# Operands of later pairs kept unsplit in DRAM, split when they are loaded at the border, and prepared at every second tick

## The chip, the cores and the metric

One core of one Trainium2 chip. The time is device microseconds of one execution of the program; the lower the better. TensorE (PE in the profile) multiplies, VectorE (DVE), ScalarE (ACT) and GpSimd (POOL) work element by element, and SyncE (SP) issues all DMAs here.

## The reference, cut to what matters

One layer of a streaming encoder on 2048 prompt tokens, 16 meta tokens and 8 x 16 sample tokens, all in float32. A mixer (retention heads and a convolution module) comes first; what the change touches is the MLP behind it.

```python
x = x + rms_norm(mix, g_post_mix)
h = rms_norm(x, g_pre_mlp)
f = jnp.square(jax.nn.relu(h @ w_mlp_in)) @ w_mlp_out      # 1024 -> 4096 -> 1024
x = x + rms_norm(f, g_post_mlp)
```

## The kernel before, in words

**Splits.** Every float32 operand of a matmul is split into a rounded part (fp32r, made by an ACT copy) and the rest (made by a subtraction on POOL or DVE); `split` (L325) does both. A product is then three matmuls: high by high, high by low, low by high (`mm3`, L451; `product`, L1125).

**Groups, pairs, blocks.** The tokens lie in six groups; the mixer works group by group. The MLP works on three pairs of groups, `FG = [(1, 2), (3, 4), (5, 0)]`, numbered G = 0, 1, 2, with 2 x 384, 2 x 384 and 2 x 320 columns (`NH2`). For each pair it goes through 16 blocks `b` of the hidden layer (`plan`, L88; the loop at L1257). A block computes layer 1 as a 2 x 2 block product in seven products P1 to P7 instead of eight (Winograd's form): seven left operands made of sums of weight blocks (`wp`, `fetch_product`, L268), and seven right operands made of sums of activation blocks (`hops`, called `op` in the profile). Each product is 12 matmuls (4 k, three each) and accumulates in three PSUM tiles `mm`. Between the products stand the 16 tiles of layer 2 of the block before (`l2_tile`, L1189, six matmuls each). In the last block of pairs 0 and 1 layer 2 of that block follows at once (`end_layer2`, L1204, 16 more tiles), and block 0 of the next pair has products alone. This change of pairs is called the border here.

**Weights.** For pair 0 the seven `wp` of a block are summed on POOL, split on ACT (L298) and POOL (L299) and stored to DRAM (L319, `wprod`); for pairs 1 and 2 they are loaded from there (L273). Layer 2's weights are loaded and split anew for each pair (`split_unit`, L254: L258 to L261). Both share nine buffers, and `next_unit` (L305) fetches ahead as far as they go.

**Right operands.** Seven tiles, each of eight column blocks: four k high, four k low. Their places (`home`, L541) are tiles that the mixer used before. The operands of pair 0 are made in place by `make_h2` with `put_home` (L547, L576). Those of pairs 1 and 2 are prepared during the pair before by the generator `prologue` (L1065): first `mlp_in` for each of the two groups (L476: residual add, two RMS norms, each in a pass of eight steps that loads one block of 128 channels, with a norm between; results `x1d` and `hd` in DRAM), then `make_h2` with `put_dram` (L585): per k it loads `hd` into two `st` tiles (L555), forms four differences on POOL (L561), splits all seven parts into `so` tiles (L327, L328) and stores them to `opd` (L592). In the last block of the pair, right behind product x, the finished operand x of the next pair is loaded into its place by one DMA (L1142).

**What sets the order.** The program is written by generators in queues; `tick` (L367) is called after each product and after each layer 2 tile (23 times in a block with 16 tiles) and takes one step from the queue `mlp`, where `prologue` is put after block 1, and in this stage two from `norm`, which holds the epilogues. A yield of `WAIT` ends the tick for its queue. Before the last block `mlp` is drained. A planner in the framework then places the instructions in the engines' queues by a simulated timeline, in which steps of `mlp` are set back by 100 places (`later`, L337) and those of `norm` by none; each engine's queue runs in its order. `st` tiles come from a pool of three (L1056), `s` tiles from a pool of five (L473), the PSUM tiles of `mlp_in`'s norms from the pool `aux` that layer 2 uses as well.

Of the kernel before, what the change touches and what calls it, by code (L numbers as in the profile page):

```python
# [12 lines left out]
F32 = mybir.dt.float32  # L13
F32R = mybir.dt.float32r
I32 = mybir.dt.int32
AF = mybir.ActivationFunctionType
ALU = mybir.AluOpType
# [3 lines left out]
P = 128  # L21
# [60 lines left out]
P1, P2, P3, P4, P5, P6, P7 = range(7)  # L82
ORDER = (P1, P2, P6, P5, P7, P3, P4)
NG = 3
NH2 = [384, 384, 320]
# [66 lines left out]
def build(nc, T):  # L152
    lg = _log_gamma()
    with tile.TileContext(nc, schedule_with_timeline_sim=True) as tc, ExitStack() as top:
# [12 lines left out]
        dram = ep(tc.tile_pool(name="dram", bufs=1, space=DRAM))  # L167
# [157 lines left out]
        def split(src, hi, lo, eng=None):  # L325

            nc.scalar.activation(out=hi, in_=src, func=AF.Copy)  # L327
            (eng or nc.gpsimd).tensor_tensor(out=lo, in0=src, in1=hi.bitcast(F32), op=ALU.subtract)  # L328
# [4 lines left out]
        queues = {"head": deque(), "norm": deque(), "conv": deque(), "mlp": deque()}  # L333

        rate = {"norm": 1, "conv": 5, "mlp": 1}
# [3 lines left out]
        def advance(gen, off):  # L339

            tc.cur_priority += off
            try:
                return next(gen)
            finally:
                tc.cur_priority -= off

        def step(name, n):
            q = queues[name]
            while n > 0 and q:
                try:  # L350
                    if advance(q[0], later["ln" if q[0].__name__ == "conv_norm" else name]) == WAIT:
                        return
                    n -= 1
                except StopIteration:
                    q.popleft()

        heads_done = {}

        def tick_heads():
            hq = queues["head"]  # L360
            for gen in list(hq):
                try:
                    advance(gen, later["head"])
                except StopIteration:
                    hq.remove(gen)

        def tick():  # L367
            tick_heads()
            step("norm", rate["norm"])
            step("conv", rate["conv"])  # L370
            step("mlp", rate["mlp"])

        def drain(*names):
            while any(queues[n] for n in names):
# [85 lines left out]
        NM = max(g["N"] for g in LAY)  # L460
# [6 lines left out]
        hd = [dram.tile([KT, P, 2 * n], F32, name=f"hd{G}") for G, n in enumerate(NH2)]  # L467
        stqs = []

        def st_tile():  # L470
            return stqs[0].tile([P, 2 * NM], F32, tag="st", name="st")

        def s_tile(N):  # L473
            return np_.tile([P, WM], F32, tag="s", name="s", bufs=SB)[:, :N]
# [61 lines left out]
        OPS = (P1, P2, P6, P5, P7, P3, P4)  # L536
        HOME = {P1: "hhi", P2: "hlo", P6: "chi", P5: "clo", P7: "x", P3: "hhi", P4: "hlo"}
        hops, h2_made = {}, set()
        opd = [None] + [dram.tile([7, P, 8 * n], F32, name=f"opd{n}") for n in NH2[1:]]

        def home(G, x):  # L541
            pool = {"h": hp, "c": catp, "x": xp}[HOME[x][0]]
            t = pool.tile([P, 8, NM if pool is catp else WM], F32R, tag=HOME[x], name=f"op{x}")
            hops[G, x] = t[:, :, :NH2[G]]
            return hops[G, x]
# [36 lines left out]
                yield  # L582
            return put

        def put_dram(G, eng):  # L585
            n = NH2[G]

            def put(x, k, part):
                t = stqs[0].tile([P, 2, NM], F32R, tag="so", name="so", bufs=2)[:, :, :n]
                split(part, t[:, 0], t[:, 1], eng)  # L590
                yield
                nc.sync.dma_start(opd[G][x].rearrange("p (h k n) -> p h k n", h=2, k=4)[:, :, k], t.bitcast(F32))  # L592
            return put


        mstack = ExitStack()
# [199 lines left out]
        part = {}  # L796
# [268 lines left out]
        def prologue(G):  # L1065
            for gi in FG[G]:
                yield from mlp_in(gi)
            yield from make_h2(G, OPS, nc.gpsimd, put_dram(G, nc.gpsimd))

        def segments(G, c):  # L1070

# [46 lines left out]
        def layer1(G, b):  # L1118

            n = NH2[G]  # L1120
            fh = [fp.tile([P, FB, NM], F32R, tag=f"fh{c}", name=f"fh{c}") for c in range(2)]
            fl = [fp.tile([P, FB, NM], F32R, tag=f"fl{c}", name=f"fl{c}") for c in range(2)]
            banks = {}

            def product(x, key, first, last=True):  # L1125
                while (G, x) not in h2_made:
                    step("norm", 1)
                w = next_unit("p", G, (b, x))
                ops = hops[G, x]
                if first:  # L1130
                    banks[key] = mmp.tile([P, 512], F32, tag="mm", name="mm")[:, :n]
                ps = banks[key]
                for k in range(4):
                    hi, lo = w[:, k * P:(k + 1) * P], w[:, 512 + k * P:512 + (k + 1) * P]
                    start = first and k == 0
                    nc.tensor.matmul(ps, hi, ops[:, k, :n], start=start, stop=False, skip_group_check=not first)  # L1136
                    nc.tensor.matmul(ps, hi, ops[:, 4 + k, :n], start=False, stop=False, skip_group_check=not first)  # L1137
                    nc.tensor.matmul(ps, lo, ops[:, k, :n], start=False, stop=(k == 3), skip_group_check=not first)  # L1138
                if b == NFB - 1 and G < NG - 1:

                    t = home(G + 1, x)
                    nc.sync.dma_start(t.bitcast(F32), opd[G + 1][x].rearrange("p (k n) -> p k n", k=8))  # L1142
                    h2_made.add((G + 1, x))
                return ps

            def copy(ps):
                t = x1p.tile([P, NM], F32, tag="sn", name="sn", bufs=2)[:, :n]
                nc.scalar.activation(out=t, in_=ps, func=AF.Copy)
                return t

            def added(ps, t):
                r = yop.tile([P, NM], F32, tag="yo", name="c", bufs=3)[:, :n]
                nc.vector.tensor_tensor(out=r, in0=ps, in1=t, op=ALU.add)
                return r

            def out(i, c, src, r=None):

                if r is None:
                    r = yop.tile([P, NM], F32, tag="yo", name="r", bufs=3)[:, :n]
                    nc.scalar.activation(out=r, in_=src, func=AF.Relu)  # L1160
                    nc.vector.scalar_tensor_tensor(out=r, in0=src, scalar=0.0, in1=r, op0=ALU.max, op1=ALU.mult)
                else:
                    nc.scalar.activation(out=r, in_=r, func=AF.Relu)
                    nc.scalar.activation(out=r, in_=r, func=AF.Square)
                split(r, fh[c][:, i, :n], fl[c][:, i, :n])

            def run():
                s1 = copy(product(P1, "y", True))
                yield
                r = added(product(P2, "z", True), s1)  # L1170
                out(0, 0, None, r)
                yield
                u2 = copy(product(P6, "y", False))
                yield
                product(P5, "w", True)
                yield
                u3 = copy(product(P7, "y", False))
                r = added(banks["w"], u3)
                out(1, 1, None, r)
                yield  # L1180
                r = added(product(P3, "w", False), u2)
                out(0, 1, None, r)
                yield
                out(1, 0, product(P4, "y", False))
                yield

            return (fh, fl), run()
# [69 lines left out]
        for G, b, steps in plan():  # L1257
            if b == 0:
                drain("norm")
                ya = {(c, r): x1p.tile([P, 4, NM], F32, tag=f"ya{c}{r}", name=f"ya{c}{r}")  # L1260
                      for c in range(2) for r in range(2)}
            rate["norm"] = 2
            if b == NFB - 1:
                drain("mlp")
            cur, run = layer1(G, b)
            w = {}
            for what, x in steps:
                if what == "p":
                    next(run)
                    tick()  # L1270
                elif what == "w":
                    w[x] = next_unit("l2", G, x)
                else:
                    q, o, c = x
                    l2_tile(G, b - 1, c, q, o, w[b - 1, q], prev, ya)
                    tick()
            if b == 1 and G + 1 < NG:
                queues["mlp"].append(prologue(G + 1))
            if b == NFB - 1:
                if G + 1 < NG:  # L1280
                    end_layer2(G, b, [w[b, q] for q in range(FB)], cur, ya)
                else:
                    last_layer2(G, [w[e, q] for e in (b - 1, b) for q in range(FB)], (prev, cur), ya)
            prev = cur
# [59 lines left out]
```

## Time and profile before

| what | us |
|---|---|
| median of 3 runs | 2510.81 |
| lowest and highest of them | 2507.74, 2510.89 |
| the profiled execution, its own time | 2508.38 |
| its span, first to last instruction | 2506.6 |

The MLP of pair 0 begins at about 975 us of the span, the border to pair 1 lies at about 1485 to 1535 us, that to pair 2 at about 2010 to 2060 us. The page gives for every engine its busy time, and a chain of what released what, followed back from the last instruction. A window row gives, for one stretch, the busy time of each engine and in brackets how many instructions ran in it, then TensorE's granted clock as a share of 2.4 GHz, the busy share of the 16 DMA engines and what they moved. A matmul's shown time overlaps with its neighbours', so the count of matmuls in a stretch tells more than their busy time. A group row gives the busy time, the mean of one in ns, and behind the second bar the idle time just before, with what ended it.

### The profile page before, as it was taken

Reading aid. Unit: us, or ns where it says so; the run is one execution under the profiler, and the core shown is the slowest. Engines: PE = TensorE matmul, PEld = TensorE weight load, DVE = VectorE, ACT = ScalarE, POOL = GpSimd, SP = SyncE. Lnnn points to the kernel's source line nnn. Section 1 sums busy time; section 2 is a strip of 40 time slices with the busy share of each in tenths; the row PEclk is TensorE's granted clock in tenths of the full one; section 3 lists DMA queues with packets and bytes.
Section 4 is the critical chain, followed back from the end, with each engine's and each line's share of the span. In section 5 each row is a group of like instructions: output and inputs, shape, how many; then the busy total and the mean of one; then the engine's idle time right before and its main releaser. Section 6 shows DMA issues by size and latency. Waiting matters only on the chain. (4 is left out here: it accounts for less than half of the span.)

```text
span 2506.6 us, 40862 instructions
## 1 busy us (share of the span) xinstructions
PE 2383.7 (95%) x14538; PEld 2340.0 (93%) x14538; DVE 1473.2 (59%) x3292; ACT 894.8 (36%) x1896; POOL 1111.9 (44%) x1024
## 2 busy tenths in 40 slices
PE   7889999998999998998999999989999999999997
PEld 6789999998999997987999999989999999999996
DVE  8879797896987955555433337554333355333335
ACT  5424424123233234444444444333422233333232
POOL 6625212131232115775999764435622226233324
PEclk8999999998999999998999999999999999999999
DMA  9888778898597778676877569778744487555552
GB/s 335 319 284 318 254 271 268 247 326 273 196 306 261 245 255 336 230 258 229 285 265 273 187 231 358 256 231 270 262 152 151 152 298 270 184 177 187 175 189 90
DMA packets 257628, 617.43 MB, mean 246 GB/s; under 512 B 32144, under 2 KB 116880, under 8 KB 256528
## 3 DMA queue, kind: packets, MB, share of 16 engines
q1 hardware_dynamic: 257424, 614.82, 71.9%
q8 instruction: 115, 1.88, 0.3%
q14 instruction: 89, 0.73, 0.1%
HBM read 463.69 MB, written 151.02 MB: 245 GB/s over the span
## 5 line engine op out<-in xcount | busy, mean ns | idle before, releaser
L1136 PE MATMUL mm<-op,wp 128*128 128x384 f32 (+1 forms) x1344 | 444.6, 333 | 22.6 <-ACT wp L298 10.1
L1138 PE MATMUL mm<-op,wp 128*128 128x384 f32 (+1 forms) x1344 | 443.6, 331 | 6.2 <-POOL wp L299 6.2
L1137 PE MATMUL mm<-op,wp 128*128 128x384 f32 (+1 forms) x1344 | 443.9, 330 | 1.4 <-DVE op L328 1.4
L260 POOL TENSOR_TENSOR wlo<-raw,whi 128x512 fp32r<-128x512 f32 x244 | 320.7, 1334 | 270.2 <-PE mma L456 117.5
L745 DVE SCALAR_TENSOR_TENSOR cv<-ext,par,cv 128x384 f32<-128x384 f32 (+1 forms) x720 | 379.2, 568 | 1.7
L454 PE MATMUL mm<-hhi,whi 128*128 128x384 f32 (+2 forms) x992 | 336.2, 339 | 18.7 <-ACT whi L259 9.7
L456 PE MATMUL mm<-hhi,wlo 128*128 128x384 f32 (+2 forms) x992 | 333.9, 338 | 10.7 <-POOL wlo L260 5.8
L455 PE MATMUL mm<-hlo,whi 128*128 128x384 f32 (+2 forms) x992 | 332.4, 335 | 0.3
L1201 DVE TENSOR_TENSOR ya<-mmc,ya 128x384 f32<-128x384 f32 (+1 forms) x344 | 181.8, 535 | 241.5 <-PE mmc L456 240.5
L1201 DVE TENSOR_TENSOR ya<-mma,ya 128x384 f32<-128x384 f32 (+1 forms) x344 | 183.5, 534 | 231.6 <-PE mma L456 231.1
L328 POOL TENSOR_TENSOR fl<-c,fh 128x384 fp32r<-128x384 f32 (+1 forms) x144 | 144.5, 1005 | 324.4 <-ACT fh L327 303.7
L1136 PEld LDWEIGHTS mm<-op,wp 128*128 128x128 f32 x1344 | 255.8, 191 | 30.4 <-ACT wp L298 13.5
L1138 PEld LDWEIGHTS mm<-op,wp 128*128 128x128 f32 x1344 | 256.0, 191 | 8.6 <-POOL wp L299 8.5
L1137 PEld LDWEIGHTS mm<-op,wp 128*128 128x128 f32 x1344 | 256.5, 191 | 2.5 <-DVE op L328 2.2
L456 PE MATMUL mmc<-fh,wlo 128*128 128x384 f32 (+1 forms) x768 | 252.2, 330 | 6.0 <-POOL wlo L260 6.0
L454 PE MATMUL mma<-fh,whi 128*128 128x384 f32 (+1 forms) x768 | 252.4, 331 | 4.7 <-DVE ya L1201 2.4
L454 PE MATMUL mmc<-fh,whi 128*128 128x384 f32 (+1 forms) x768 | 251.4, 330 | 4.0 <-DVE ya L1201 3.2
L455 PE MATMUL mmc<-fl,whi 128*128 128x384 f32 (+1 forms) x768 | 251.9, 328 | 0.9 <-POOL fl L328 0.8
L455 PE MATMUL mma<-fl,whi 128*128 128x384 f32 (+1 forms) x768 | 251.6, 328 | 0.3 <-POOL fl L328 0.3
L456 PE MATMUL mma<-fh,wlo 128*128 128x384 f32 (+1 forms) x768 | 251.3, 327 | 0.4 <-POOL wlo L260 0.4
L454 PEld LDWEIGHTS mm<-hhi,whi 128*128 128x128 f32 x992 | 194.1, 196 | 21.2 <-ACT whi L259 11.1
L456 PEld LDWEIGHTS mm<-hhi,wlo 128*128 128x128 f32 x992 | 192.8, 195 | 15.0 <-POOL wlo L260 8.7
(237 smaller groups left out, 4810.4 us busy)
## 6 DMA issues: line engine op xcount, KB each, us to landing
wp<-wprod SPq DMA_DIRECT2D x224, 512.0 KB, 4.2
raw<-w SPq DMA_DIRECT2D x256, 256.0 KB, 4.1
whi<-wkeep_in SPq DMA_DIRECT2D x120, 512.0 KB, 5.9
wlo<-wkeep_in SPq DMA_DIRECT2D x120, 512.0 KB, 4.9
wprod<-wp SPq DMA_DIRECT2D x112, 512.0 KB, 4.4
whi<-wkeep_out SPq DMA_DIRECT2D x40, 512.0 KB, 6.3
wlo<-wkeep_out SPq DMA_DIRECT2D x40, 512.0 KB, 5.6
s<-yscr SPq DMA_DIRECT2D x80, 192.0 KB, 4.4
```

The source lines that it names most:

```text
L260: (nc.vector if i < 24 and i % 4 == 0 else nc.gpsimd).tensor_tensor(out=lo[:, c], in0=raw, in1=hi[:, c].bitcast(F32), op=ALU.subtract)
L328: (eng or nc.gpsimd).tensor_tensor(out=lo, in0=src, in1=hi.bitcast(F32), op=ALU.subtract)
L454: nc.tensor.matmul(ps, whi(k), ahi(k), start=(k == 0), stop=False)
L455: nc.tensor.matmul(ps, whi(k), alo(k), start=False, stop=False)
L456: nc.tensor.matmul(ps, wlo(k), ahi(k), start=False, stop=(k == nk - 1))
L745: nc.vector.scalar_tensor_tensor(out=o, in0=src(t), scalar=wt, in1=o, op0=ALU.mult, op1=ALU.add)
L1136: nc.tensor.matmul(ps, hi, ops[:, k, :n], start=start, stop=False, skip_group_check=not first)
L1137: nc.tensor.matmul(ps, hi, ops[:, 4 + k, :n], start=False, stop=False, skip_group_check=not first)
L1138: nc.tensor.matmul(ps, lo, ops[:, k, :n], start=False, stop=(k == 3), skip_group_check=not first)
L1201: last_y[0] = nc.vector.tensor_tensor(out=y, in0=ps, in1=y, op=ALU.add)
```

## The change

The seven operands of a later pair are no longer split and stored while the pair before runs. Four of them are differences, which `differences` forms on POOL and stores unsplit to `td`; the other three are blocks of `hd` as they are. In the last block, behind product x, a generator `reload` for operand x is put into the queue `norm`: it loads the four unsplit k blocks by two DMAs into two `st` tiles, then splits them into the operand's place, the copy on ACT, the subtraction in turn on POOL and DVE. The prologue is put into its queue after block 2 instead of block 1, and from then on `mlp` gets a step at every second tick.

```diff
+        ticks, slow = [0], [1]
...
-            step("mlp", rate["mlp"])
+            ticks[0] += 1
+            if ticks[0] % slow[0] == 0:
+                step("mlp", rate["mlp"])
...
-        opd = [None] + [dram.tile([7, P, 8 * n], F32, name=f"opd{n}") for n in NH2[1:]]
+
+        td = [None] + [dram.tile([4, 4, P, n], F32, name=f"td{n}") for n in NH2[1:]]
...
-        def put_dram(G, eng):
+        def differences(G):
+
             n = NH2[G]
-
-            def put(x, k, part):
-                t = stqs[0].tile([P, 2, NM], F32R, tag="so", name="so", bufs=2)[:, :, :n]
-                split(part, t[:, 0], t[:, 1], eng)
-                yield
-                nc.sync.dma_start(opd[G][x].rearrange("p (h k n) -> p h k n", h=2, k=4)[:, :, k], t.bitcast(F32))
-            return put
+            for k in range(4):
+                bs = {}
+                for r in range(2):
+                    t = st_tile()[:, :2 * n]
+                    nc.sync.dma_start(t, hd[G][k + 4 * r])
+                    bs[r, 0], bs[r, 1] = t[:, :n], t[:, n:]
+                yield
+                ts = []
+                for i in range(4):
+                    x, y = ((bs[0, 1], bs[0, 0]), (bs[1, 1], ts[0] if i == 1 else None), (bs[1, 1], bs[0, 1]),
+                            (bs[1, 0], ts[1] if i == 3 else None))[i]
+                    t = s_tile(n)
+                    nc.gpsimd.tensor_tensor(out=t, in0=x, in1=y, op=ALU.subtract)
+                    nc.sync.dma_start(td[G][i, k], t)
+                    ts.append(t)
+                    yield
+
+        def reload(G, x):
+
+            n = NH2[G]
+            t = home(G, x)
+            ld = []
+            for k in (0, 2):
+                src = {P1: lambda: hd[G][k:k + 2, :, :n], P2: lambda: hd[G][4 + k:6 + k, :, :n],
+                       P3: lambda: hd[G][4 + k:6 + k, :, n:], P5: lambda: td[G][0, k:k + 2],
+                       P6: lambda: td[G][1, k:k + 2], P7: lambda: td[G][2, k:k + 2],
+                       P4: lambda: td[G][3, k:k + 2]}[x]()
+                ld.append(st_tile()[:, :2 * n].rearrange("p (k n) -> p k n", k=2))
+                nc.sync.dma_start(ld[-1], src.rearrange("k p n -> p k n"))
+            yield
+            for k in range(4):
+                split(ld[k // 2][:, k % 2], t[:, k], t[:, 4 + k], nc.vector if k % 2 else nc.gpsimd)
+                if k == 3:
+                    h2_made.add((G, x))
+                yield
...
-            yield from make_h2(G, OPS, nc.gpsimd, put_dram(G, nc.gpsimd))
+            yield from differences(G)
...
-
-                    t = home(G + 1, x)
-                    nc.sync.dma_start(t.bitcast(F32), opd[G + 1][x].rearrange("p (k n) -> p k n", k=8))
-                    h2_made.add((G + 1, x))
+                    queues["norm"].append(reload(G + 1, x))
...
-            if b == 1 and G + 1 < NG:
+            if b == 2 and G + 1 < NG:
+                slow[0] = 2
                 queues["mlp"].append(prologue(G + 1))
```

## Rows read from the trace of the kernel before

**Rows 1.** The page: span, TensorE's busy time, chain that ended last by engine.

```profile
span 2506.6 us, 40862 instructions
...
PE 2383.7 (95%) x14538; PEld 2340.0 (93%) x14538; DVE 1473.2 (59%) x3292; ACT 894.8 (36%) x1896; POOL 1111.9 (44%) x1024
...
PE 27%; DMA 3%; POOL 1%; DVE 1%; issue 0%; ACT 0%; SPq 0%; DVEq 0%; ACTq 0%; POOLq 0%
```

**Rows 2.** Windows: 100 us in pair 0 and 100 us in pair 1, undisturbed.

```profile
core 0: us, PE busy (x) PEld busy (x) DVE busy (x) ACT busy (x) POOL busy (x), PEclk, DMA share, GB/s
...
1260.00:1360.00 100.00, 100.00 (x579) 100.00 (x578) 34.29 (x65) 48.10 (x98) 98.00 (x87) 1.00 0.74 264
...
1835.00:1935.00 100.00, 100.00 (x579) 100.00 (x578) 35.00 (x64) 28.40 (x56) 28.39 (x25) 1.00 0.46 148
```

**Rows 3.** Windows: stretches of the prologues of pair 1 and pair 2.

```profile
1035.00:1110.00 75.00, 73.40 (x414) 71.32 (x413) 42.76 (x82) 35.37 (x73) 55.84 (x49) 1.00 0.72 243
1110.00:1210.00 100.00, 82.62 (x389) 74.71 (x388) 53.42 (x98) 36.40 (x74) 61.68 (x54) 0.88 0.77 255
...
1560.00:1660.00 100.00, 97.08 (x547) 94.14 (x545) 61.56 (x118) 36.41 (x75) 44.00 (x40) 1.00 0.80 263
1660.00:1735.00 75.00, 64.30 (x335) 60.75 (x336) 37.14 (x82) 24.56 (x54) 32.07 (x34) 0.95 0.71 229
1785.00:1810.00 25.00, 22.88 (x132) 22.42 (x131) 7.33 (x14) 10.66 (x23) 15.26 (x17) 1.00 0.81 268
```

**Rows 4.** Groups of TensorE's matmuls, 1110 to 1210 us, with their waits.

```profile
L1136 PE MATMUL mm<-op,wp 128*128 128x384 f32 x60 | 23.7, 394 | 7.7 <-ACT wp L298 7.7
L1138 PE MATMUL mm<-op,wp 128*128 128x384 f32 x60 | 22.8, 386 | 3.0 <-POOL wp L299 3.0
...
L456 PE MATMUL mmc<-fh,wlo 128*128 128x384 f32 x30 | 11.2, 392 | 3.7 <-POOL wlo L260 3.7
```

**Rows 5.** The same groups, 1660 to 1735 us, then 1785 to 1812 us.

```profile
L1136 PE MATMUL mm<-op,wp 128*128 128x384 f32 x51 | 18.7, 366 | 8.3 <-DMA wp<-wprod 6.7 <-DVE st L397 1.6
...
L454 PE MATMUL mma<-fh,whi 128*128 128x384 f32 x12 | 4.1, 345 | 2.1 <-ACT fh L327 2.1
```

**Rows 6.** Groups of POOL and of ACT, 1200 to 1360 us: the splits into `so`.

```profile
L328 POOL TENSOR_TENSOR so<-s,so 128x384 fp32r<-128x384 f32 x16 | 17.4, 1094 | 0.0
L328 POOL TENSOR_TENSOR so<-st,so 128x384 fp32r<-128x384 f32 x12 | 13.0, 1082 | 0.0
...
L327 ACT ACTIVATE so<-s 128x384 fp32r<-128x384 f32 x16 | 8.3, 521 | 17.5 <-DMA opd<-so 15.9 <-POOL so L328 1.6
...
L327 ACT ACTIVATE so<-st 128x384 fp32r<-128x384 f32 x12 | 6.2, 519 | 4.6 <-DMA opd<-so 3.4 <-DMA st<-hd 1.3
```

**Rows 7.** DMA issues of the whole kernel: KB each, median us from issue to landing.

```profile
st<-hd SPq DMA_DIRECT2D x32, 384.0 KB, 5.6
opd<-so SPq DMA_DIRECT2D x28, 384.0 KB, 4.0
op<-opd SPq DMA_DIRECT2D x7, 1536.0 KB, 13.6
```

**Rows 8.** Tile `s` and line 561: ns of one (min/median/max), DVE and POOL.

```profile
L524 POOL TENSOR_TENSOR s<-s x48: 725/1013/1330, 504.5 to 1699.0; 128x384 f32<-128x384 f32 x40, 128x256 f32<-128x256 f32 x8
...
L522 DVE SCALAR_TENSOR_TENSOR s<-s,par,sw x32: 471/606/617, 1067.3 to 1696.7; 128x384 f32<-128x384 f32 x24, 128x256 f32<-128x256 f32 x8
...
L561 POOL TENSOR_TENSOR s<-st x16: 869/955/1136, 1201.6 to 1784.0; 128x384 f32<-128x384 f32 x8, 128x320 f32<-128x320 f32 x8
```

**Rows 9.** Pair 0's operands: their splits, then DVE's group and the window 985 to 1010.

```profile
L327 ACT ACTIVATE op<-s x16: 508/524/527, 930.4 to 1011.9; 128x384 fp32r<-128x384 f32 x16
L328 DVE TENSOR_TENSOR op<-s,op x16: 546/559/1357, 930.9 to 1012.5; 128x384 fp32r<-128x384 f32 x16
...
L327 ACT ACTIVATE op<-st x12: 507/517/528, 928.3 to 1006.3; 128x384 fp32r<-128x384 f32 x12
...
L328 DVE TENSOR_TENSOR op<-s,op 128x384 fp32r<-128x384 f32 x3 | 3.2, 1083 | 1.2 <-ACT op L327 1.2
...
985.00:1010.00 25.00, 17.53 (x73) 14.47 (x71) 18.90 (x16) 11.48 (x23) 25.00 (x18) 0.80 0.92 334
```

**Rows 10.** Window in pair 0 without a prologue.

```profile
1410.00:1435.00 25.00, 25.00 (x146) 25.00 (x145) 9.26 (x17) 11.39 (x22) 19.32 (x17) 1.00 0.63 209
```

**Rows 11.** Windows of 5 us around single waits of TensorE.

```profile
1115.00:1120.00 5.00, 2.15 (x9) 1.83 (x10) 0.26 (x1) 0.63 (x1) 2.65 (x3) 0.87 0.79 251
1120.00:1125.00 5.00, 4.67 (x15) 4.16 (x14) 2.55 (x5) 0.00 (x0) 3.02 (x3) 0.50 0.91 273
...
1640.00:1645.00 5.00, 3.47 (x20) 3.15 (x19) 4.87 (x11) 0.36 (x1) 2.68 (x2) 1.00 0.96 370
```

**Rows 12.** Windows of the two borders.

```profile
1485.00:1535.00 50.00, 50.00 (x288) 49.73 (x287) 25.70 (x50) 17.14 (x34) 15.81 (x14) 1.00 0.96 380
...
2010.00:2060.00 50.00, 50.00 (x293) 49.73 (x292) 23.61 (x46) 16.87 (x35) 14.16 (x13) 1.00 0.91 322
```

## The prediction

> **What bounds the kernel.** The page comes first: TensorE is busy 95% of the span, and the chain that ended last is mostly matmuls [rows 1]. So only time in which TensorE stands still, or runs slowly, can be won. Where that is, the windows of the MLP stage show. In an undisturbed stretch 100 us hold 579 matmuls of 384 columns, 0.1727 us each, beside no idle time at clock 1.00, in the first pair as in the second [rows 2]. A block `b` is 180 of them (84 in the products, 96 in layer 2), 31.1 us. Stretches in which the next pair's operands are prepared hold fewer [rows 3]. What is missing, against 5.79 per us, by 0.1727 us:
> - first prologue, group 3: 434 - 414 = 20, 3.5 us; group 4: 579 - 389 = 190, 32.8 us
> - second prologue, group 5: 579 - 547 = 32, 5.5 us; group 0: 434 - 335 = 99, 17.1 us; the end of its operands: 145 - 132 = 13, 2.2 us
>
> That is 61.1 us in all. TensorE's idle time in these five rows is 1.60 + 17.38 + 2.92 + 10.70 + 2.12 = 34.7 us; the other 26.4 us are matmuls at the lower clock (rows 3: granted 0.88 and 0.95 in the two worst). What it waits for is weights: in the first pair operands that ACT and POOL still have to split, in the second a `wp` load that SP issued late [rows 4, 5]. These engines' queues run in order, and the steps of `mlp_in` stand between: a load, then DVE, POOL, ACT and a store, each waiting for the one before. In group 4's stretch neither DVE, ACT nor POOL is busy two thirds of the time [rows 3]: it is blocked order, not a full engine.
>
> **What is removed.** For each later pair 28 ACT copies, 28 POOL subtractions and 28 stores of 384 KB and 7 loads of 1536 KB (a sixth less for the last pair) [rows 6, 7]. In the first prologue that is 14.5 us of ACT and 30.4 us of POOL, but it lies between 1200 and 1360 us, and from 1260 on TensorE loses nothing there though POOL is busy 98 of 100 us [rows 2, 6]: weights fetched ahead cover a full POOL. So the removal itself is worth the 2.2 us at 1785 to 1810, where TensorE waited for an `fh` split on ACT [rows 5]. If the cover goes, it is worth more; nothing here says so.
>
> **What is moved and thinned.** `mlp_in` is 28 steps a group (8, 2, 8, 2, 8), two groups; `make_h2` 4 x 8 = 32; `differences` 4 x 5 = 20. So 88 steps become 76, and at every second tick they take 152 ticks for 88. A block has 23 ticks: 6.6 blocks (206 us) for 3.8 (119 us). It begins one block later and ends around block 10, well ahead of the drain at block 15. The later start leaves the first blocks alone, where 73 of 145 matmuls were done in 25 us, 12.4 us missing [rows 9]; those wait for the first pair's own splits, so I count nothing, and up to a quarter, 3 us, for the range. In the middle pass of `mlp_in` one step costs DVE 0.61 and 0.56 us, POOL 1.01 us [rows 8, 9] (the second DVE operation is an add of the same width as the DVE splits, whose duration I take). At a step per tick (31.1 / 23 = 1.35 us) DVE gets 0.87 of its time on top of the 0.35 that the blocks need [rows 2], more than it has; POOL in the first pair gets 0.75 on top of 0.77 [rows 10]. At half the rate this is 0.43 + 0.35 on DVE and 0.37 + 0.77 on POOL, in a pass of eight steps a backlog of 3 us. A load is also issued one step ahead of its use, and a step becomes 2.7 us long.
>
> How much of the 61.1 us returns no row shows. Below: nothing (the waits keep their size; a loss I exclude, since each queue gets less in any stretch). Above: all of it. The nearest rows are the prologues' own first groups, same operations at the same rate, which lose 3.5 and 5.5 us before queues are behind. I take that each second group falls to its first group's loss: 2 x (3.5 + 5.5) = 18.0 us stay, **43.1 us return**. The clock's part goes with it: at 1640 to 1645 us a lone 1.53 us of idle time left the clock at 1.00, while at 1115 to 1125 idle time in close order brought it down to 0.50, which is 1.2 GHz [rows 11].
>
> The Trainium skill, "TensorE: Matmul & The Clock Gate", section "A second HAM failure mode: psum-queue depth-cycling", says that frequent short idles between groups of matmuls are enough to bring the lower clock, paid for again each time; the second of these rows agrees, the first does not. By it the same number of waits over twice the stretch would win nothing, and the sum would be 2512: rival 2.
>
> **What is added.** At each of two borders 14 loads, 28 ACT copies, 14 POOL and 14 DVE splits. ACT: 28 x 0.52 = 14.6 us; POOL 14 x 1.09 = 15.3 us; DVE 14 x 0.56 = 7.8 us, or 14 x 1.08 = 15.1 us as in the stretch where POOL was busy throughout [rows 6, 9]. The borders' 50 us leave ACT 33, POOL 34 and DVE 24 us free while TensorE has no idle time [rows 12]. So the price is not room but order. An operand's place is free once its product in the last block is done; a reload then stands on ACT and POOL in front of the `fh` and `fl` splits that layer 2 of the last block waits for, and its loads stand on SP in front of `wp` and `raw`. I take one reload in front of that split: 4 x 0.52 + 1.09 = 3.2 us a border, **6.3 us** for both; it could be nothing (the planner can put a product of the next pair there), or, if reloads come too slowly, 26 us a border (below). DMA gets lighter: 14 loads of 384 KB, 5.4 MB, in place of 7 of 1536 KB, 10.8 MB, at a border that had a DMA share of 0.96 [rows 12]; priced at nothing. `differences` keeps the 16 POOL differences of a pair [rows 8] and adds 16 stores of 192 KB; each waits on SP for its difference, with `wp` loads behind it, as the 28 stores waited for their splits.
>
> **Sum.** 61.1 - 18.0 - 6.3 = 36.8 us from the profiled execution's own 2508.4 us (span 2506.6 and 1.8 around it): 2471.6, said as **2472**. The median of the three runs, 2510.81, lies 2.4 us higher, inside what the sum can tell.
>
> **Rivals.**
> 1. *The waits keep their idle time, the clock alone comes back.* Every step blocks for its DMA's time however far apart steps are; 34.7 us of idle time stay but scattered, 26.4 return: 2508.4 - 26.4 + 6.3 = **2488**. For: every wait is a latency. Against: group 3 had the same steps and lost a tenth of group 4.
> 2. *Nothing returns.* The waits keep size and number, and the clock falls as often: 2508.4 - 2.2 + 6.3 = **2512**. It also comes out so if the planner, which places instructions by its own estimate of when they are ready, draws the thinned steps together again. For: the row with 0.50. Against: the lone gap there.
> 3. *The border is laid open: slower.* The only rows with 28 splits into these places, those of the first pair, took from 928 to 1012 us, 12 us an operand, and TensorE was busy 17.53 of the last 25 [rows 9]. At a border the reload of the first operand can begin 2 us into the last block, and the seventh is wanted at 31.1 + 16.6 (the last layer 2) + 12.4 = 60 us; that allows 8.3 us an operand. At 12 us the seventh is ready at 86: 26 us late, 52 for both, 2508.4 - 43.1 + 52 = **2517**, and up to 2535 with the lower clock and late first operands. Against: at the borders no block's `wp` are still to be split as at the start, the weights of the next pair being loaded, and the ticks issue an operand every 4.4 us. For: only three `st` buffers serve the loads, two an operand, so loads (5.6 us [rows 7]) and splits (2.1 us of ACT) may follow one another: 7.7 us, close under 8.3.
>
> **How the numbers follow.** Forecast 0.50, rival 1 0.20, rival 2 0.10, rival 3 0.20. The forecast's own range goes from 2444 (all 61.1 us back, no price, and 3 us of the start) to 2491 (two borders at 13 us, half the worst); with rival 1 and rival 2 the range is **2444 to 2513**, which leaves out about rival 3. About 0.2% (5 us) is what a measurement can tell from no change. Forecast and rival 1 are faster by more: 0.70; rival 2 is the same: 0.10; slower 0.20.
>
> **What would show it.** Right: no window of the prologues below 130 matmuls in 25 us, clock 1.00 from 1060 to 1480 us and in the second pair; `mlp_in` steps over some 200 us; TensorE's waits for `wp` in rows 4 and 5 under a third; the border windows at 140 or more in 25 us. Wrong: windows with 75 to 110 matmuls still there, only further apart (rivals 1, 2); TensorE waiting for ACT or DVE writing `op`, or for `st` loads, at the first block of a pair (rival 3).

## The result, and the profile after

| kernel | median us | lowest to highest | ratio to before (95% interval) |
|---|---|---|---|
| before | 2509.27 | 2507.70 to 2510.89 | |
| changed | 2470.64 | 2467.02 to 2475.32 | 0.9847 (0.9825 to 0.9868) |

2472 was forecast. The profiled execution of the changed kernel took 2468.89 us (span 2467.0), 39.5 us less than that of before (2508.38); 36.8 us were forecast.

The page of the changed kernel, next to [rows 1]: TensorE has the same 14538 matmuls, is busy 20.6 us less with them, and the span is 39.6 us shorter; so about half of the gain is idle time, and the rest a shorter busy time for the same matmuls.

```profile
span 2467.0 us, 40738 instructions
...
PE 2363.1 (96%) x14538; PEld 2327.8 (94%) x14538; DVE 1506.2 (61%) x3320; ACT 894.5 (36%) x1896; POOL 1092.7 (44%) x996
```

Where the 39.5 us went is a matter of counting matmuls, as with [rows 2, 3]. Two stretches that hold both prologues in either kernel, but for their first loads, 325 and 250 us, would hold 1882 and 1448 matmuls at 5.79 per us. First the kernel before:

```profile
1035.00:1360.00 325.00, 306.02 (x1667) 296.04 (x1666) 149.35 (x279) 142.52 (x287) 265.52 (x232) 0.96 0.75 260
1560.00:1810.00 250.00, 234.26 (x1301) 227.31 (x1300) 123.65 (x247) 90.68 (x192) 123.87 (x125) 0.99 0.78 256
```

The same windows of the changed kernel, then the worst stretch of before [rows 3] in it, and the two parts of its prologues in which most of the rest is missing:

```profile
1035.00:1360.00 325.00, 318.55 (x1824) 315.56 (x1823) 164.94 (x295) 143.37 (x283) 265.91 (x224) 1.00 0.75 259
1560.00:1810.00 250.00, 245.60 (x1391) 241.93 (x1390) 126.11 (x248) 82.81 (x170) 96.84 (x92) 0.99 0.70 232
...
1110.00:1210.00 100.00, 96.34 (x547) 94.21 (x545) 63.27 (x111) 49.74 (x101) 82.98 (x71) 1.00 0.83 284
...
1135.00:1260.00 125.00, 118.55 (x671) 115.83 (x671) 82.94 (x144) 55.56 (x111) 99.08 (x84) 1.00 0.85 294
...
1635.00:1660.00 25.00, 22.72 (x117) 21.82 (x118) 14.99 (x31) 9.71 (x20) 12.77 (x12) 0.93 0.81 266
```

Before, 215 and 147 matmuls are missing; after, 58 and 57. That is (157 + 90) x 0.1727 = 42.7 us returned, and 115 x 0.1727 = 19.9 us that stay. The reader should see that DVE, ACT and POOL are busy as long in the first window as before, or longer (149 and 165, 143 and 143, 266 and 266 us): there it is not an engine standing freer that won the time. The first pair's worst stretch of before, with 389 matmuls at a clock of 0.88, holds 547 at 1.00.

The borders, the same 100 us from the last block's start on: the kernel before, pair 0 to 1 and pair 1 to 2, then the changed kernel.

```profile
1485.00:1585.00 100.00, 99.86 (x573) 99.01 (x572) 59.28 (x107) 38.39 (x77) 51.30 (x46) 1.00 0.91 335
2013.00:2113.00 100.00, 99.07 (x619) 97.69 (x618) 59.89 (x113) 35.34 (x76) 47.86 (x43) 1.00 0.92 320
```

```profile
1460.00:1560.00 100.00, 97.94 (x557) 96.02 (x556) 72.10 (x122) 47.46 (x99) 66.00 (x57) 1.00 0.79 266
1972.00:2072.00 100.00, 99.03 (x621) 97.98 (x620) 69.72 (x127) 46.68 (x105) 60.11 (x57) 1.00 0.78 266
```

The first border lost 16 matmuls, 2.8 us; the second none. 42.7 - 2.8 = 39.9 us, against the 39.5 us between the two profiled executions.

What TensorE still waits for, by its groups, 1135 to 1260 us and then 1635 to 1735 us of the changed kernel, next to [rows 4, 5]:

```profile
L1170 PE MATMUL mm<-op,wp 128*128 128x384 f32 x94 | 31.5, 337 | 0.5 <-DVE c L1184 0.5
L458 PE MATMUL mma<-fh,whi 128*128 128x384 f32 x70 | 24.5, 350 | 5.3 <-DVE ya L1232 4.0 <-DVE s L534 1.2
...
L1170 PE MATMUL mm<-op,wp 128*128 128x384 f32 x83 | 28.6, 347 | 2.5 <-DMA wp<-wprod 2.5
```

The waits for weights of the first pair (7.7, 3.0 and 3.7 us) are gone; what is left there is DVE, mostly late in emptying a layer 2 PSUM tile (4.0 us), and late with a norm step that holds a PSUM tile of the same pool (L534, 1.2 us). In the second pair the wait for a late `wp` load fell from 6.7 to 2.5 us.

### The profile page after: what moved, and what is told of

Read it like the earlier page. It is cut to its first block, busy times and chain, and to the rows that moved or that the text cites. A ratio compares the mean times of both kernels' runs of the same rounds, so it can differ in the third digit from the quotient of the medians.

```text
span 2467.0 us, 40738 instructions
## 1 busy us (share of the span) xinstructions
PE 2363.1 (96%) x14538; PEld 2327.8 (94%) x14538; DVE 1506.2 (61%) x3320; ACT 894.5 (36%) x1896; POOL 1092.7 (44%) x996
## 4 chain that ended last, share of the span: by engine, by line
PE 69%; DVE 14%; DMA 9%; POOL 3%; issue 3%; ACT 2%; SPq 1%; DVEq 0%; POOLq 0%; ACTq 0%
PE mm L1170 7%; PE mm L1171 7%; PE mm L1172 7%; PE mm L460 6%; PE mm L459 6%; PE mm L458 6%; PE mmc L459 4%; PE mmc L460 4%; PE mma L458 4%; PE mmc L458 4%; PE mma L459 4%; PE mma L460 4%; DVE cv L779 4%; DMA s<-yscr 3%; DMA st<-hd 1%
## 5 line engine op out<-in xcount | busy, mean ns | idle before, releaser
L458 PE MATMUL mm<-hhi,whi 128*128 128x384 f32 (+2 forms) x992 | 333.6, 337 | 19.9 <-ACT whi L259 10.3
```

The source lines that it names most:

```text
L458: nc.tensor.matmul(ps, whi(k), ahi(k), start=(k == 0), stop=False)
```

## The experiments

The before beside these runs had medians of 2500.7 to 2504.4 us on their chips, so kernels are compared by ratios, and by times only where they shared a chip.

**One half of the change each: `spread_only` and `unsplit_only`.** The first is the kernel before with the thinning alone, the second the changed kernel without it:

```diff
 spread_only, against before
+            ticks[0] += 1
+            if ticks[0] % slow[0] == 0:
+                step("mlp", rate["mlp"])
...
-            if b == 1 and G + 1 < NG:
+            if b == 2 and G + 1 < NG:
+                slow[0] = 2

 unsplit_only, against the changed kernel
-            if b == 2 and G + 1 < NG:
-                slow[0] = 2
+            if b == 1 and G + 1 < NG:
```

> The kernel before with the thinning alone (start after block 2, one prologue step at every second tick); operands still split and stored to DRAM early and loaded by one DMA at the border. Theory A, the thinning of the norm steps makes the gain: both prologues lose about 15 us in place of 61, and the border keeps the price of before, so 2463 to 2472 us, at or slightly under the changed kernel. Theory B, the removed splits and stores make the gain: 2500 to 2510 us.

> The changed kernel with the rate and the start of before: operands unsplit and reloaded at the border, prologue step at every tick after block 1. Theory A: only the 2 us of the operand stage come back and the border costs up to 6 us, 2504 to 2514 us; windows with 75 to 110 matmuls in 25 us are there again in the second group of each prologue. Theory B: 2470 to 2485 us, no such windows.

Measured: `spread_only` 2465.97 us, ratio 0.9844 (0.9822 to 0.9867); `unsplit_only` 2504.92 us, 1.0008 (0.9994 to 1.0021), before beside both 2503.08. Theory A holds and B falls: the thinning alone, with the start one block later, makes the whole gain, and keeping the operands unsplit alone makes none that can be measured. The windows of `spread_only`, the same two stretches:

```profile
1035.00:1360.00 325.00, 319.06 (x1825) 315.90 (x1825) 165.25 (x294) 151.43 (x302) 279.04 (x239) 1.00 0.75 264
1560.00:1810.00 250.00, 245.34 (x1403) 242.49 (x1402) 124.88 (x246) 92.21 (x193) 114.06 (x113) 1.00 0.71 239
```

1825 against the changed kernel's 1824 in the first pair, with all the splits still there. And `unsplit_only`, its second groups' stretches and its first border:

```profile
1110.00:1210.00 100.00, 81.67 (x394) 74.17 (x394) 54.33 (x99) 36.11 (x73) 62.83 (x55) 0.90 0.77 260
...
1660.00:1735.00 75.00, 66.57 (x351) 62.38 (x350) 40.03 (x88) 23.02 (x50) 27.75 (x30) 0.95 0.72 235
...
1485.00:1585.00 100.00, 93.64 (x522) 91.54 (x521) 73.22 (x114) 47.60 (x100) 62.72 (x56) 0.98 0.71 238
```

394 and 351 stand where before had 389 and 335: the loss is all but untouched. The border of this execution holds 522 matmuls against 573, 8.8 us, more than the 20 matmuls (3.5 us) that its two prologue stretches hold beyond before's.

**Is it the density, or a debt of the first group? `pause_full_rate` and `late_full_rate`.** The prediction took the second groups' loss for a queue that the first group leaves behind. Both kernels take a norm step at every tick; one takes 46 empty steps, two blocks, behind each of the two groups, the other only starts two blocks later:

```diff
 pause_full_rate, against unsplit_only
             for gi in FG[G]:
                 yield from mlp_in(gi)
+                for _ in range(46):
+                    yield

 late_full_rate, against unsplit_only
-            if b == 1 and G + 1 < NG:
+            if b == 3 and G + 1 < NG:
```

> The kernel unsplit_only (prologue step at every tick) with 46 empty steps, two blocks, after each group's norm steps. The prediction took the loss of the second group to be a queue left behind by the first. If that is so, the pause lets the queues catch up and each second group loses about as little as its first (3 to 6 us): 2466 to 2478 us although every step is as dense as before. If the density inside a group makes the loss, the second groups lose as much as ever: 2498 to 2510 us.

> The kernel unsplit_only (a prologue step at every tick, no pause) begun two blocks later, after block 3. In pause_full_rate the second group ran two blocks later and lost nothing. If its place in the pair was what helped, the late start helps as well: 2470 to 2485 us. If it was the rest between the groups, the second groups lose as much as in unsplit_only, only two blocks later: 2498 to 2510 us.

Measured: with the rest 2465.5 us, 0.9842 (0.9822 to 0.9862), half a microsecond under the range that was expected of a queue left behind; with the late start 2502.62 us, 1.0005 (0.9986 to 1.0023). First group and second group of both pairs with the rest, each from the first to the last load of its norm passes (the first pair's first group from its sixth load on, since five are fetched early):

```profile
1039.00:1122.70 83.70, 82.08 (x464) 79.86 (x463) 48.48 (x90) 38.07 (x77) 64.39 (x55) 1.00 0.73 247
1127.30:1224.30 97.00, 97.00 (x558) 96.34 (x557) 58.11 (x109) 48.06 (x96) 80.03 (x67) 1.00 0.79 276
...
1549.80:1624.70 74.90, 73.28 (x415) 71.49 (x414) 47.21 (x92) 30.16 (x63) 31.87 (x30) 1.00 0.81 277
1625.10:1721.90 96.80, 95.10 (x548) 94.51 (x547) 51.78 (x107) 32.49 (x71) 35.95 (x34) 1.00 0.67 219
```

The groups of the first pair in `unsplit_only`, and the second group in the changed kernel, by the same bounds:

```profile
1035.60:1120.40 84.80, 80.09 (x445) 76.89 (x443) 47.88 (x88) 36.88 (x75) 63.70 (x54) 0.99 0.72 245
1121.40:1194.80 73.40, 59.75 (x278) 53.85 (x278) 40.98 (x76) 28.18 (x57) 42.14 (x37) 0.88 0.72 242
```

```profile
1162.00:1243.40 81.40, 76.72 (x435) 74.91 (x434) 52.58 (x94) 38.37 (x79) 65.29 (x55) 1.00 0.83 283
```

With the rest the second group of the first pair lacks 4 matmuls against 5.79 per us, in `unsplit_only` 147 (25.4 us), with a step at every tick in both. The late start shows the same hole two blocks later:

```profile
1185.00:1210.00 25.00, 19.19 (x86) 16.94 (x85) 13.14 (x23) 9.85 (x20) 13.57 (x12) 0.86 0.64 219
1210.00:1235.00 25.00, 16.56 (x65) 13.30 (x63) 10.19 (x19) 9.42 (x19) 15.67 (x14) 0.82 0.76 251
```

So it is not the rate of the ticks alone, nor the place in the pair, but that two groups follow without rest. The rest alone buys what the half rate buys. Whether a debt of the first group is the reason is not shown, because the rest also changed how dense the second group stands in the trace. Its loads do not wait for two blocks; they begin 4.6 us behind the first group's last and then take longer. Without the time that TensorE lost in them, the second group's loads take 73.4 - 25.4 = 48.0 us in `unsplit_only`, where the first group's take 76.9; they take 75.1 in the changed kernel and 96.4 with the rest. A second group that is packed too densely fits these rows as well as a queue left behind by the first, and no run tells them apart.

**What makes the loss: `prefetch2` and `no_sum_adds`.** Both at full rate, without rest. One loads two steps ahead (in the later pairs' steps only) and into four tiles of its own instead of the pool of five `s` tiles, the other leaves DVE work out (for k of 2 to 7 the squares are not summed, so the norms' statistics are of two blocks only):

```diff
 prefetch2, against unsplit_only
-                ahead = []
-                for k in range(KT + 1):
+                ahead, far = [], 1 if early else 2
+                for k in range(KT + far):
...
-                        y = s_tile(N)
+                        y = s_tile(N) if early else stqs[0].tile([P, NM], F32, tag="ls", name="ls", bufs=4)[:, :N]
...
-                    if k:
+                    if k >= far:

 no_sum_adds, against unsplit_only
-            else:
+            elif not late:
                 (eng or nc.vector).tensor_tensor(out=acc, in0=acc, in1=sq[:, :W], op=ALU.add)
...
-                add_square(acc, y, k, N)
+                add_square(acc, y, k, N, late=not early)
```

> The kernel unsplit_only at full rate, its norm passes loading two steps ahead instead of one, into four tiles of their own. If the dense stretch loses because a load is issued too short a time before its use, the loss in the second groups falls to under half: 2478 to 2492 us. If it loses because the chain DVE, POOL, ACT and the engines' own queues are overfilled, loading earlier wins little: 2498 to 2512 us.

> The kernel unsplit_only at full rate with the DVE adds that sum the squares of a later pair's norms left out for k of 2 to 7 (the statistics are then of two blocks only). If DVE, filled over its time in the dense passes, is what falls behind, a quarter of DVE's work in the passes less brings the loss of the second groups under half: 2470 to 2488 us. If the loss is order and latency, it stays: 2495 to 2510 us.

Measured: `prefetch2` 2494.5 us, 0.9963 (0.9950 to 0.9977), between the two ranges that were expected; `no_sum_adds` 2474.75 us in a single run, so without an interval, its before 2504.43. The second groups, `prefetch2` first, then `no_sum_adds`:

```profile
1110.00:1210.00 100.00, 89.09 (x457) 83.51 (x456) 59.97 (x109) 39.48 (x79) 69.31 (x59) 0.93 0.82 284
...
1660.00:1735.00 75.00, 71.06 (x391) 69.08 (x392) 39.78 (x86) 22.80 (x50) 38.17 (x41) 0.98 0.79 273
```

```profile
1110.00:1210.00 100.00, 93.23 (x507) 90.02 (x506) 55.29 (x96) 44.67 (x89) 81.99 (x70) 0.97 0.87 308
...
1660.00:1735.00 75.00, 74.28 (x424) 73.05 (x423) 32.89 (x65) 20.62 (x41) 35.37 (x36) 1.00 0.80 279
```

394 became 457 with earlier loads and 507 with a lighter DVE; 351 became 391 and 424. Over the two whole stretches (1035 to 1360 and 1560 to 1810 us) 342 matmuls were missing in `unsplit_only`, 241 with the earlier loads and 155 with the lighter DVE. Loads that come late, or the tiles that they wait for, are about a third of it; DVE's adds are more than half. The adds that were left out also shorten the chain from ACT to DVE, so this does not tell a full DVE from a long chain through it; DVE was busy 54 of the 100 us in `unsplit_only`, which speaks for the chain.

**How far thinning goes: `slow3`, `spread_third`, `after_prefetch2`, `after_again`.** `slow3` is the changed kernel and `spread_third` is `spread_only`, both with `slow[0] = 3`; `after_prefetch2` adds the two steps of prefetch to the changed kernel; `after_again` is the changed kernel.

> The changed kernel with a prologue step at every third tick. If the remaining 15 us of loss in the prologues come from density (theory A), a third less density takes some 5 us more off: 2462 to 2468 us. If every step has a wait of its own that no thinning removes (rival), the loss stays: 2468 to 2474 us. Slower than 2476 us only if the two PSUM banks that the norms hold for longer cost layer 2 more.

> The kernel spread_only (operands still split early, one load at the border) with a prologue step at every third tick. 88 steps take 264 ticks, 11.5 blocks, which ends just before the drain. It has no reload at the border and the thinnest prologue: 2455 to 2463 us if density and border are the two remaining costs; like spread_only (2464 to 2468 us) if the remaining waits belong to single steps.

> The changed kernel with the norm passes loading two steps ahead. At half rate a load is already issued 2.7 us ahead; the prefetch won 10 us at full rate. If part of the remaining 15 us of loss is still load latency, 2458 to 2466 us; if it is DVE order alone, no difference from the changed kernel (within 3 us).

> The changed kernel itself, on the chip of the runs beside it, to compare them and spread_only by their ratios: 0.983 to 0.986.

Measured: `slow3` 2464.01 us, 0.9844 (0.9822 to 0.9866), beside `spread_only`'s 2465.97; `spread_third` 2457.65 us, 0.9832 (0.9815 to 0.9848); `after_prefetch2` 2462.1 us, 0.9830 (0.9812 to 0.9848), and `after_again` on the same chip 2467.25 us, 0.9854 (0.9834 to 0.9875). The window of the first prologue in `slow3`, then both in `after_prefetch2`:

```profile
1035.00:1360.00 325.00, 321.99 (x1834) 318.84 (x1833) 164.87 (x294) 147.33 (x287) 266.02 (x224) 0.99 0.74 257
```

```profile
1035.00:1360.00 325.00, 321.75 (x1843) 318.73 (x1842) 163.64 (x297) 145.47 (x286) 265.32 (x224) 1.00 0.74 260
1560.00:1810.00 250.00, 249.10 (x1428) 247.08 (x1427) 129.23 (x255) 84.97 (x174) 98.08 (x94) 1.00 0.69 232
```

A third of the rate finds 10 more matmuls in the first prologue, the prefetch 19 and, in the second, 37: 56 x 0.1727 = 9.7 us of the 19.9 that were left. Such a count differs between executions: the two kernels below have the prologues of `after_prefetch2`, which held 1843 and 1428, and held 1845 and 1828 in the first stretch, 1431 and 1429 in the second. So the 37 stand out, while the 10 do not, nor do the ratios tell a third of the rate from half of it. In time the medians of `after_prefetch2` and the changed kernel differ by 5.2 us, and their runs on that chip do not overlap (2460.1 to 2463.0, 2464.7 to 2473.1), though the intervals of the ratios do. Of the versions run it is, with `spread_third`, the fastest by ratio, but the two kernels below, with the same prefetch, came to 0.9849 and 0.9850: a gain of the prefetch in time is not shown.

**What the border costs: `pf_reload_pool` and `pf_reload_dve`.** The groups of DVE at the changed kernel's first border, 1455 to 1530 us, answer to [rows 9]:

```profile
L328 DVE TENSOR_TENSOR op<-st,op 128x384 fp32r<-128x384 f32 x14 | 15.1, 1086 | 14.2 <-ACT op L327 14.1
```

A DVE subtraction took 1086 ns, on average, with POOL at work beside every one of the 14, and DVE stood idle 14.1 us in front of them for ACT's copies. `after_prefetch2` was run with these subtractions all on one engine, POOL as shown in `pf_reload_pool`, DVE (`nc.vector`) in `pf_reload_dve`:

```diff
-                split(ld[k // 2][:, k % 2], t[:, k], t[:, 4 + k], nc.vector if k % 2 else nc.gpsimd)
+                split(ld[k // 2][:, k % 2], t[:, k], t[:, 4 + k], nc.gpsimd)
```

> The kernel after_prefetch2 with all 28 reload subtractions of a border on POOL instead of half on DVE. At the first border of the changed kernel the 14 DVE splits took 15.1 us and held DVE's queue idle for 14.1 us more, and TensorE's waits there name DVE. If that is the border's price (4 to 9 us at the first border), it falls to under half: 2456 to 2460 us where after_prefetch2 is 2462. If POOL's queue is the tighter one (14 us more work before the fl splits), slower: 2464 to 2470 us.

> The same with all 28 subtractions on DVE. If DVE's queue is what the border costs, the price of the first border doubles: 2465 to 2474 us. If only the ACT copies and loads in front count, no change from after_prefetch2 (2460 to 2464 us).

Measured: 2461.09 us, 0.9849 (0.9829 to 0.9868), and 2462.43 us, 0.9850 (0.9833 to 0.9866). They do not differ, and neither gains on `after_prefetch2`. But `pf_reload_dve` did not double DVE's time, on which its range rested. DVE's group of `pf_reload_dve`, 1455 to 1530 us:

```profile
L328 DVE TENSOR_TENSOR op<-st,op 128x384 fp32r<-128x384 f32 x28 | 20.2, 753 | 9.4 <-ACT op L327 9.4
...
L328 DVE TENSOR_TENSOR op<-st,op x28: 541/554/1664, 1458.1 to 1493.3; 128x384 fp32r<-128x384 f32 x28
```

With no subtractions of the reload on POOL, half of DVE's took 554 ns or less; the eighteen that ran while POOL did nothing took 541 to 559. So 28 took 20.2 us where 14 took 15.1, and with the idle time in front of them DVE spent 29.6 us on the reload, as against 29.3. So this run cannot tell whether DVE's queue is the border's price. `pf_reload_pool`, with no subtractions on DVE, could; its time lies between the two ranges that were expected. The first border over 100 us, in eight executions with the reload and two without, with TensorE's waits there for DVE to empty a layer 2 tile (`ya`):

| execution of | window | matmuls | fewer than before's 573, us | waits for `ya`, us |
|---|---|---|---|---|
| `spread_only`, no reload | 1455 to 1555 | 573 | 0 | 0 |
| `spread_third`, no reload | 1455 to 1555 | 560 | 2.2 | 0 |
| changed | 1460 to 1560 | 557 | 2.8 | 0.6 |
| `after_again` | 1460 to 1560 | 534 | 6.7 | 3.1 |
| `unsplit_only` | 1485 to 1585 | 522 | 8.8 | 4.4 |
| `slow3` | 1455 to 1555 | 540 | 5.7 | 3.1 |
| `pause_full_rate` | 1460 to 1560 | 541 | 5.5 | 2.2 |
| `after_prefetch2` | 1455 to 1555 | 540 | 5.7 | 2.7 |
| `pf_reload_dve` | 1460 to 1560 | 551 | 3.8 | 3.2 |
| `pf_reload_pool` | 1470 to 1570 | 561 | 2.1 | 0 |

So with the reload 2 to 9 us are missing at the first border, differing from one execution to the next of the same kernel (2.8 and 6.7), and up to 2.2 without it; nothing is missing at the second, where pair 1 has no `wp` to split. TensorE mostly waits longest for DVE where most is missing, and in `pf_reload_pool` that wait is gone. That speaks for DVE's queue as the larger part of the price; with one execution of each kernel and ratios that do not differ it is not shown.

## Why the prediction was right, point by point

- **What bounds it.** Right: both prologues, in the named stretches, held the gain. 42.7 us returned there; the prediction said 43.1. 19.9 us stayed; it said 18.0. That these sums are so close is in part luck: by the bounds of the loads the four groups of the changed kernel lost 1.4, 6.3, 5.9 and 2.3 us, where 3.5, 3.5, 5.5 and 5.5 were forecast, and some 4 us lie outside them.
- **Why the second group is worse.** "Queues are behind" was an assumption, taken to let the first group's loss stand for what stays. The rest and the late start show that the second group loses because it follows the first at once; that it is queues left behind, and not its own density in the trace, they do not show.
- **The removal is worth the 2.2 us.** Right in kind: `unsplit_only` counted 8 matmuls more than before in the first prologue (1675 against 1667), 12 in the second (1313 against 1301), 3.5 us together, though executions of the same first prologue differ by up to 17 above, and in time it was not seen (1.0008). The forecast's cover, weights fetched ahead of a full POOL, held: in `spread_only` POOL was busy 279 of 325 us with the same matmuls.
- **The thinning.** That thinner steps return the time was right; how the ticks thin them was not. But for five loads fetched early, the loads of the norm passes run from 1035.5 to 1195.3 us before and from 1067.9 to 1243.4 after, the start one block (32.4 us) later, as was said. The two stretches, and POOL's eight adds of the first group's middle pass, before and then after:

```profile
1035.50:1195.30 159.80, 141.95 (x721) 132.28 (x721) 89.03 (x165) 65.16 (x132) 106.15 (x91) 0.93 0.73 243
...
L524 POOL TENSOR_TENSOR s<-s x8: 1003/1014/1019, 1068.3 to 1098.3; 128x384 f32<-128x384 f32 x8
```

```profile
1067.90:1243.40 175.50, 170.29 (x970) 167.62 (x969) 109.06 (x192) 82.87 (x168) 141.85 (x119) 1.00 0.77 264
...
L528 POOL TENSOR_TENSOR s<-s x8: 1014/1023/1030, 1112.8 to 1139.1; 128x384 f32<-128x384 f32 x8
```

Without the 35.3 and 8.0 us that TensorE lost in there this is 124.5 and 167.5 us of work, 1.3 times, not twice. The 56 norm steps of a prologue were reckoned at 76 and 152 us: the steps of before already ran far behind their ticks. Within the middle pass nothing was thinned, an add every 4.3 us before and every 3.8 after, where 1.35 and 2.7 were reckoned; there the steps stand together as rival 2 feared. What grew is the time between passes (from the last load of the first pass to the middle pass's next loads, 1045.8 to 1071.9 us before and 1076.1 to 1116.7 after) and the second group. So DVE's and POOL's demand at 1.35 us a step, 0.87 and 0.75 of their time, did not stand in that pass, and it was the wrong measure as well: `pause_full_rate` kept the rate of the ticks and lost 5.9 us in each prologue, where `unsplit_only` lost 35.7 and 23.3.
- **The clock.** The split into 34.7 us idle and 26.4 us at the lower clock was too neat: by the granted clock of 0.88 over 100 us and 0.95 over 75 us [rows 3] the clock cost 12.0 + 3.8 = 15.8 us, and some 10 us were in neither. After, 10.9 us of idle time stand beside 19.9 us missing, at a granted clock of 1.00 and 0.99: some 9 us are missing in neither. Rival 1, by which all 34.7 us of idle time stay, fell with that. What the forecast needed held in the profiled execution: with the waits scattered, the granted clock is 1.00 in every 25 us window of the first prologue; the one fall in the two prologues, to 0.93, is at 1635 to 1660 us behind a single wait of 1.9 us for `wp`, so a lone wait did bring the clock down here, unlike the 1.53 us of [rows 11]. In the dense stretch of before the clock fell to 0.50 behind several waits in close order [rows 11]. The Trainium skill, "TensorE: Matmul & The Clock Gate", section "A second HAM failure mode: psum-queue depth-cycling", tells of a clock that falls and rises again where TensorE often stands idle for a short time between groups of matmuls. The row of the dense stretch agrees with it.
- **The border.** 6.3 us were forecast, 3.2 a border; it was 2.8 at the first in the profiled execution and nothing at the second. That is one execution; `after_again`, the same kernel, lost 6.7 us at the first border. The DVE price of 1.08 us and the 15.1 us were right to the digit. The step that the 3.2 us stood for, a reload in front of the `fh` and `fl` splits, was not what TensorE waited for: it waited 1.4 us for a `wp` load and 0.6 us for DVE. Rival 3, the border laid open, did not come: the splits of the reloads ran between 1458 and 1495 us, and TensorE did not wait for an `op`.
- **The signs.** No prologue window under 130 matmuls: one had 117. The clock at 1.00: in the first pair, not in one window of the second. Steps over some 200 us: 175.5 in the first prologue from the sixth load on, 202.7 in the second. The waits for `wp` under a third: none in the first pair, 2.5 of 6.7 us in the second, which is under a third of the sum alone. Border windows of 140 or more: 139 and 135 were the lowest. So most signs held, and the windows, the clock and the border each missed in one or two places.

The sum came out at 36.8 for 39.5 us: the prologues' return was put 0.4 us too high and the border's price 3.5 us too high. In `after_again` the same counts give 41.4 us returned and 6.7 us lost at the first border, so both terms move by more than these errors from one execution to the next.

## What to carry to other kernels

Work off the critical path that waits step by step for DMAs and other engines can cost TensorE little in a first batch and much in a second that follows without rest: count matmuls per window to find where, and try a pause before thinning or moving work. Then read from the trace how dense the work stands; the rate at which the program hands it out does not tell. Removing work that such a stretch hides is worth at most what its window lacks, here 2 to 4 us by count and nothing in time for 56 stores and 112 instructions, however much it takes off an engine's busy time. A change of two parts should be measured in halves; here one half is the whole gain, and the other can be left out.

## What the runs showed that was not expected

A rest of 46 steps behind each group at the full rate, 0.9842, did as much as half the rate at every step, 0.9847. And putting all 28 subtractions of a border on DVE cost DVE no more time than half of them: each took 753 ns on average instead of 1086, with 541 to 559 where POOL stood still, and 29.6 us went on them with their idle time, as against 29.3.
